# A third weight chunk ahead of x, smaller first loads, and small matmuls among the rows of a one-core decoder layer

## The chip, the cores and the metric

The kernel runs on one core of a Trainium2 chip. The metric is the device time of one execution in microseconds (us), the median over the runs shown. TensorE does the matrix products, VectorE (DVE in the profile), ScalarE (ACT) and GpSimd (POOL) the elementwise work; SyncE (SP) issues most of the loads. Each engine takes its instructions strictly in the order in which they stand in its own list and waits on semaphores for the others.

## The reference

One layer of a decoder trunk on 256 tokens of width 1024, with 256 memory tokens, all in float32:

```
h = rms_norm(x, norm_mix_g)                       # mean of squares, sqrt, reciprocal, gain
x = x + hybrid_mixer(h, ...)                      # h @ w_in -> conv module (u), NSA attention (q, kc, vc, ...), gates; @ w_out
h = rms_norm(x, norm_x_g)
x = x + cross_attention(h, mem, xq_w, xkv_w, xo_w)
#   q = h @ wq; k, v = split(mem @ wkv); p = softmax(q k^T / sqrt(256)) over 4 heads; o = (p v) @ wo
h = rms_norm(x, norm_ffn_g)
x = x + swiglu(h, ffn_in_w, ffn_out_w)
return rms_norm(x, final_norm_g)
```

The keys of the cross-attention, `mem @ wkv`, need only `mem`. So the kernel computes them first, while `x` is still being loaded and normalised.

## The kernel before

**Tiles.** Activations are held transposed, as 8 blocks of 128 channels by 256 tokens. The weights come in chunks of 256 columns (1 MB), each loaded in two halves of 512 KB. `k0` to `k3` are the four chunks of the cross-attention's keys, `u0` to `u7` the conv module's, then `kc`, `vc`, `q0` and so on; `xq0` to `xq3` and `xo0` to `xo3` are the cross-attention's query and output chunks, `f0` to `f21` those of the FFN. In the names of the profile the chunk's number is left out: `k_0h` is the high part of half 0 of some k chunk.

**Splitting.** A float32 operand is split in two parts that TensorE multiplies fast: `split` (L174 and after) lets ScalarE copy the half to a rounded high part (L184) and VectorE subtract that from it to get the low part (L186). From `u1` to the gates' first chunk GpSimd does the subtraction instead. `part` (L301 to L304) does the same for activations: `memh`, `meml` from `mem_t`; `hh`, `hl` from `hf`; `kxh`, `kxl` from a finished k bank.

**Matmuls.** `rows` (L248 to L262) multiplies one half of a chunk: three rows of 8 matmuls, 128x128 by 128x256 each, namely high weights by high activations, high by low, low by high. A chunk so takes 48 matmuls of L259. Only `k0` is multiplied in plain float32 (`whole`, L289), straight from the loads.

**The start.** After 8 warm-up products (L364), TensorE does `k0`, then `k1`, then the norm of x: `rooted_all` (L343 to L351) multiplies the squares of x, folded to two blocks on VectorE (L399), by a matrix of ones (L347, the bank `rn`); ScalarE takes the root (L349), VectorE the reciprocal (L350), then eight products give `hf` (L405) in four pairs, and each pair is split (`part`) to `hh`, `hl`. Then the rest of `k2`, `k3` and the u chunks follow. Loads are issued by SP in the order of the calls: `k0`, `k1`, x in two halves, two tables (`cpt`, `ppt`), `k2`, `k3`, `u0`; `mem_t` is loaded from ScalarE's queue.

**What sets the order.** A scheduler with a model of the engines puts the instructions of each engine in order ahead of the run. The kernel bounds it by marks: `first[name]` (L178) says after which instruction a chunk may be split, `in_line` (L240) chains rows of TensorE, and from `xq0` to the xo chunks `in_turn` (from L1038) writes the order out by hand.

**Cross-attention.** The scores' scale is the norm of the new x, which `rnorm(acc1, "2", 256.0)` (L329 to L341, bank `rn`) makes from two small products with 2 columns (L333), a root and a reciprocal. It is called ahead of `in_turn` (L980), its result `r16` is first used behind the first scores (`xscores(0)`, L1010, L1013).

**The small matmul.** `settle` (L244 to L246) multiplies 32 columns of an activation by 256 of it into a bank that the next chunk's first row starts afresh, so its product is thrown away. Before, it stands once, ahead of `f4`.

Of the kernel before, what the change touches and what calls it, by code (L numbers as in the profile page):

```python
# [12 lines left out]
ALU = mybir.AluOpType  # L13
# [84 lines left out]
def tile_hybrid_block(  # L98
# [56 lines left out]
    def aux(name, shape, tag, bufs):  # L155
        return axp.tile(shape, F32, tag=tag, name=name, bufs=bufs)
# [47 lines left out]
    def ahead(name, slot):  # L204

        w = held[name] = long(f"{name}w", slot, (P, NB, 256))
        if name == "k0":
            for i in range(4):
                nc.sync.dma_start(w[:, 2 * i:2 * i + 2], w0[i])
            return  # L210
        for i in range(2):
            nc.sync.dma_start(w[:, 4 * i:4 * i + 4], wst[CHUNK_AT[name]][:, 4 * i:4 * i + 4])
# [31 lines left out]
    def settle(o, x):  # L244

        nc.tensor.matmul(o[0:32], lhsT=x[:, 0:32], rhs=x, start=True, stop=True)  # L246

# [81 lines left out]
    def rnorm(sq, name, scale=1.0, tag="o"):  # L329

        ps = aux(f"rn_{name}", [P, 2, 2], tag, 1)
        for tb in range(2):
            nc.tensor.matmul(ps[:, tb], lhsT=sq[:, tb * P:tb * P + P], rhs=ones[:, 0:2], start=tb == 0, stop=tb == 1)  # L333
        r = small(f"r_{name}", [P, 2], tag="rnat", bufs=2)
        if name == "l":

            nc.vector.tensor_scalar(out=r, in0=ps[:, :, 0], scalar1=EPS, scalar2=None, op0=ALU.add)
            return newton(r, name)
        root = nc.scalar.activation(r, ps[:, :, 0], AF.Sqrt, scale=scale, bias=eps256 if scale != 1.0 else eps1)
        first[name] = root, nc.vector.reciprocal(r, r)  # L340
        return r  # L341
# [31 lines left out]
    for i in range(4):  # L373
        nc.scalar.dma_start(mem_t[:, 2 * i:2 * i + 2], memt[i])
    ahead("k0", 10)
    ahead("k1", 14)
    for i in range(2):
        nc.sync.dma_start(xt_t[:, 4 * i:4 * i + 4], xt[:, 4 * i:4 * i + 4])
    nc.sync.dma_start(cpt, cp)
    nc.sync.dma_start(ppt, pp)  # L380
    for name, slot in (("k2", 12), ("k3", 11), ("u0", 13)):
        ahead(name, slot)
# [8 lines left out]
    for i in range(2):  # L391
        hs = slice(4 * i, 4 * i + 4)
        part(memh[:, hs], meml[:, hs], mem_t[:, hs])
# [7 lines left out]
    first["k2_1"] = first["1"]  # L401
# [8 lines left out]
    for name, i in (("u0_0", 2), ("u0_1", 3), ("u1_0", 3), ("u1_1", 3)):  # L410
        first[name] = first[f"x{i}"]
# [57 lines left out]
    for j in range(NB):  # L469
        ps = gemm(f"u{j}", h)  # L470
        sg = small(f"sg{j}", [P, S], tag="sg", bufs=3)
        act = nc.scalar.activation(sg, ps[:, 1], AF.Sigmoid)
        vec = nc.vector.tensor_tensor(out=vt[j][:, PAD:], in0=ps[:, 0], in1=sg, op=ALU.mult)
        convolve(13 * (j > 0), (0, 1, 1, 1, 1, 0, 1, 1)[j], act, vec)
# [505 lines left out]
    r16 = rnorm(acc1, "2", 256.0)  # L980
    xmax, xneg, xsum = (small(n, [P, 4, 2]) for n in ("xmax", "xneg", "xsum"))
    oxh, oxl, pxh, pxl = longs(("oxh", "oxl", "pxh", "pxl"), (13, 9, 11, 12))
    px, queries = [None] * 4, [None] * 4
# [18 lines left out]
    def xscores(j):  # L1002
# [7 lines left out]
        nc.vector.scalar_tensor_tensor(out=xneg[:, j], in0=xmax[:, j], scalar=-1.0, in1=r16, op0=ALU.mult, op1=ALU.mult)  # L1010
        px[j] = small(f"px{j}", [P, 2, S], tag="vt", bufs=4)
        for qb in range(2):
            nc.scalar.activation(px[j][:, qb], s_ps[:, qb], AF.Exp, scale=r16[:, qb:qb + 1], bias=xneg[:, j, qb:qb + 1],  # L1013
                                 accum_out=xsum[:, j, qb:qb + 1])
# [25 lines left out]
    def in_turn():  # L1040
# [12 lines left out]
        some(qs[1], 3)  # L1053
        xscores(0)
        some(qs[1], 4)
# [20 lines left out]
        xo(2, 0)  # L1076
# [136 lines left out]
    homes.append(gf[:, 2:4])  # L1213
    for j in range(NF):
        ps = bank(f"ps_f{j}")
        if j == 4:
            settle(ps[:, 0], fg[:, 0, 0])
        gemm(f"f{j}", (fg[:, 0], fg[:, 1]), ps=ps)
# [279 lines left out]
```

## Time and profile before

| | us |
|---|---|
| median of 3 runs | 531.47 (531.02 to 531.73) |
| the profiled execution's own time | 532.03 |
| its span, first to last instruction | 530.0 |
| TensorE busy | 522.3 |
| VectorE, ScalarE, GpSimd busy | 433.9, 343.7, 156.0 |

The profiled execution lies 0.56 us above the median, and 2.03 us of its time lie outside the span. The mean granted clock of TensorE was 0.997. In the timeline a row is a group of instructions in a row on one engine with one form: its start, the time from its first instruction's start to its last one's end, engine, line, operation, output from inputs, and the count; in brackets the idle time ahead of it and what ended it. Matmuls overlap, so the end of a row lies past the start of the next one, and the spacing of matmuls is the difference of two rows' starts divided by the number of matmuls between them. A float32 product of L347, L289 or the warm-up shows as two records in the trace and stands once in the order.

### The profile page before, as it was taken

How to read it: one execution, taken by the hardware profiler on the slowest of the kernel's cores; microseconds unless marked ns; L12 is line 12 of the kernel's file. 1: busy time of each engine (PE TensorE's matmuls, PEld its weight loads, DVE VectorE, ACT ScalarE, POOL GpSimd, SP SyncE). 2: the span in 40 equal slices, each digit the busy share in tenths (PEclk: the TensorE clock that was granted, in tenths of full speed). 3: DMA queues.
4: the chain of work that ended last, by engine and by line, in shares of the span. 5: the costliest groups of instructions: out<-in, count | busy, mean ns of one | idle time of the engine just before them, and what ended most of it. 6: DMA issues, size and time to landing. Idle time of an engine off the chain costs nothing.

```text
span 530.0 us, 11121 instructions
## 1 busy us (share of the span) xinstructions
PE 522.3 (99%) x4316; PEld 504.8 (95%) x4316; DVE 433.9 (82%) x871; ACT 343.7 (65%) x599; POOL 156.0 (29%) x110
## 2 busy tenths in 40 slices
PE   9999999999999999999999999999999999999995
PEld 8999999999999999999999999999999999988884
DVE  4868999899978898975869676697889888878985
ACT  4685466787656888789446664665556665657553
POOL 0069999999961200200004000330000000000001
PEclk9999999999999999999999999999999999999998
DMA  8927954664355544347765643847765567455622
GB/s 309 416 98 267 350 185 161 202 216 160 121 182 177 178 141 135 105 147 213 233 205 171 235 153 119 236 167 258 218 199 198 198 233 226 157 137 173 220 88 80
DMA packets 30740, 101.55 MB, mean 192 GB/s; under 512 B 3296, under 2 KB 5856, under 8 KB 30304
## 3 DMA queue, kind: packets, MB, share of 16 engines
q1 hardware_dynamic: 29104, 96.99, 54.0%
q0 software_dynamic: 864, 2.62, 3.1%
q10 hardware_dynamic: 720, 1.23, 0.6%
q8 instruction: 34, 0.56, 0.5%
q14 instruction: 18, 0.15, 0.1%
HBM read 99.59 MB, written 1.25 MB: 190 GB/s over the span
## 4 chain that ended last, share of the span: by engine, by line
PE 60%; DVE 1%; ACT 0%; issue 0%; ACTq 0%; DVEq 0%
PE ps_f L259 23%; PE fo L1254 6%; PE ps_xo L259 4%; PE ps_v L259 4%; PE ps_pw L259 4%; PE ps_wo L259 4%; PE ps_xq L259 4%; PE m L1254 4%; PE xs L989 1%; PE xo_ps L989 1%; PE o L819 1%; PE pt_a L798 1%; PE s L753 1%; PE o L816 1%; PE pt_b L798 0%; PE o L810 0%
## 5 line engine op out<-in xcount | busy, mean ns | idle before, releaser
L437 DVE SCALAR_TENSOR_TENSOR yp<-vt,ppt,yp 128x256 f32<-128x256 f32 x204 | 81.6, 480 | 0.2
L259 PE MATMUL ps_f<-g,f_1h 128*128 128x256 f32 x352 | 44.4, 277 | 0.0
L259 PE MATMUL ps_f<-g,f_0h 128*128 128x256 f32 x352 | 43.8, 277 | 0.0
L259 PEld LDWEIGHTS ps_f<-g,f_1h 128*128 128x128 f32 x352 | 42.1, 188 | 0.1
L259 PEld LDWEIGHTS ps_f<-g,f_0h 128*128 128x128 f32 x352 | 41.8, 188 | 0.0
L184 ACT ACTIVATE f_0h<-f 128x1024 fp32r<-128x1024 f32 x22 | 23.3, 1057 | 16.8 <-issue 5.7
L186 DVE TENSOR_TENSOR f_1l<-f,f_1h 128x1024 fp32r<-128x1024 f32 x22 | 27.4, 1248 | 6.8 <-ACT f_1h L184 5.9
L184 ACT ACTIVATE f_1h<-f 128x1024 fp32r<-128x1024 f32 x22 | 23.3, 1060 | 14.3 <-PE ps_f L259 10.6
L186 DVE TENSOR_TENSOR f_0l<-f,f_0h 128x1024 fp32r<-128x1024 f32 x22 | 26.7, 1212 | 1.7 <-ACT f_0h L184 1.7
L186 POOL TENSOR_TENSOR u_0l<-u,u_0h 128x1024 fp32r<-128x1024 f32 x7 | 17.4, 2479 | 30.4 <-DVE kt L523 30.4
L259 PE MATMUL ps_f<-g,f_0l 128*128 128x256 f32 x176 | 23.9, 277 | 0.0
L259 PE MATMUL ps_f<-g,f_1l 128*128 128x256 f32 x176 | 23.7, 277 | 0.0
L259 PEld LDWEIGHTS ps_f<-g,f_0l 128*128 128x128 f32 x176 | 21.9, 188 | 0.0
L1220 DVE TENSOR_TENSOR ab<-ps_f,r 128x512 f32<-128x512 f32 x22 | 15.1, 689 | 8.3 <-PE ps_f L259 8.3
L259 PEld LDWEIGHTS ps_f<-g,f_1l 128*128 128x128 f32 x176 | 21.7, 188 | 0.0
L773 ACT ACTIVATE p<-p,mins 128x256 f32<-128x256 f32 x32 | 15.9, 502 | 8.4 <-DVE mins L758 8.4
L1138 POOL DMA_DIRECT2D spare<-in_wfo_dram x1 | 0.9, 866 | 65.1 <-DVE ab L1220 65.1
L186 POOL TENSOR_TENSOR u_1l<-u,u_1h 128x1024 fp32r<-128x1024 f32 x7 | 17.9, 2560 | 0.0
L449 POOL TENSOR_TENSOR yt<-yt,vw 128x512 f32<-128x512 f32 x13 | 17.1, 1312 | 0.0
L1222 ACT ACTIVATE sl<-ab 128x256 f32<-128x256 f32 x22 | 9.1, 417 | 11.1 <-DVE ab L1220 11.1
L1296 POOL TENSOR_TENSOR x<-y,gf 128x512 f32<-128x512 f32 x2 | 2.6, 1298 | 46.1 <-issue 46.1
L259 PE MATMUL ps_u<-hh,u_0h 128*128 128x256 f32 x128 | 16.1, 276 | 0.0
(614 smaller groups left out, 1632.1 us busy)
## 6 DMA issues: line engine op xcount, KB each, us to landing
f<-in_wst_dram SPq DMA_DIRECT2D x44, 512.0 KB, 4.3
fo<-in_wfo_dram SPq DMA_DIRECT2D x16, 512.0 KB, 3.5
u<-in_wst_dram SPq DMA_DIRECT2D x14, 512.0 KB, 7.9
q<-in_wst_dram SPq DMA_DIRECT2D x8, 512.0 KB, 4.1
ga<-in_wst_dram SPq DMA_DIRECT2D x8, 512.0 KB, 3.5
gc<-in_wst_dram SPq DMA_DIRECT2D x8, 512.0 KB, 3.7
v<-in_wst_dram SPq DMA_DIRECT2D x8, 512.0 KB, 5.8
pw<-in_wst_dram SPq DMA_DIRECT2D x8, 512.0 KB, 4.8
```

Source lines behind the costliest of these rows:

```text
L184: copy = nc.scalar.activation(hi, w, AF.Copy)
L186: splits[name] = copy, eng.tensor_tensor(out=lo, in0=w, in1=f(hi[:]), op=ALU.subtract)
L259: mm = nc.tensor.matmul(ps[:, b], lhsT=lhsT, rhs=rhs, start=row + b + kb == 0, stop=kb == NB - 1 and row == 2 and b == 1)
L437: nc.vector.scalar_tensor_tensor(out=out[:, i] if t == ts[-1] else acc[i], in0=v, scalar=w, in1=acc[i], op0=ALU.mult, op1=ALU.add)
L449: nc.gpsimd.tensor_tensor(out=yt[:, 0:2], in0=yt[:, 0:2], in1=pr, op=ALU.add)
L753: nc.tensor.matmul(s1, lhsT=qh(hd, 1), rhs=t[:, g].rearrange("p b t -> p (b t)"), start=i == 0, stop=i == 1)
L773: exp.append(nc.scalar.activation(p1[k][:, br], p1[k][:, br], AF.Exp, scale=-1.0, bias=mins[:, hd, 1, br:br + 1], accum_out=sums[:, hd, 1, ...
L798: mm = nc.tensor.transpose(ps[:, i], src, ident)
L989: mm = nc.tensor.matmul(o, lhsT=lhsT, rhs=rhs, start=n == 0, stop=n == len(order) - 1)
L1220: scaled[:] = [nc.vector.tensor_tensor(out=ab, in0=ps, in1=rf.unsqueeze(1).to_broadcast([P, 2, S]), op=ALU.mult)]
L1222: silu = nc.scalar.activation(sl, ab[:, 0], AF.Silu)
L1254: mm = nc.tensor.matmul(o, lhsT=a[x], rhs=b[w], start=start and n == 0, stop=stop and n == 2)
```

## The change

Five edits. (1) The first quarter of `mem_t` and of `k0`'s weights is each loaded as two pieces of 128 KB instead of one of 256 KB; the second half of `memh`, `meml` is split in two steps. (2) `k2` is loaded ahead of x instead of behind the tables, and its second half no longer waits for the norm's root; `u0`'s first half may be split one pair of `hf` earlier. (3) A small matmul stands among the rows of `k3`, into the bank of `u1`. (4) `r16` is made right ahead of `xscores(0)`; its bank is wider, and a small matmul goes into its second half behind the scores. (5) A small matmul stands behind the first row of `xo2`, and the one ahead of `f4` moves eight matmuls into `f3`. `settled` is `settle` chained in the line of rows.

```diff
         if name == "k0":
-            for i in range(4):
+            for k in range(2):
+                nc.sync.dma_start(w[:, k], w0[0, :, k])
+            for i in range(1, 4):
                 nc.sync.dma_start(w[:, 2 * i:2 * i + 2], w0[i])
...
+    def settled(o, x):
+
+        with in_line():
+            last[:] = [nc.tensor.matmul(o[0:32], lhsT=x[:, 0:32], rhs=x, start=True, stop=True)]
...
-    def rnorm(sq, name, scale=1.0, tag="o"):
-
-        ps = aux(f"rn_{name}", [P, 2, 2], tag, 1)
-        for tb in range(2):
-            nc.tensor.matmul(ps[:, tb], lhsT=sq[:, tb * P:tb * P + P], rhs=ones[:, 0:2], start=tb == 0, stop=tb == 1)
+    def rnorm(sq, name, scale=1.0, tag="o", beside=None):
+
+        ps = aux(f"rn_{name}", [P, 2, S], tag, 1)
+        with in_line() if beside is not None else ExitStack():
+            for tb in range(2):
+                mm = nc.tensor.matmul(ps[:, 0, 2 * tb:2 * tb + 2], lhsT=sq[:, tb * P:tb * P + P], rhs=ones[:, 0:2], start=tb == 0, stop=tb == 1)
+        if beside is not None:
+            last[:] = [mm]
+            beside.append(ps[:, 1])
+        ps = ps[:, 0, 0:4].rearrange("p (t c) -> p t c", t=2)
...
-    for i in range(4):
+    for k in range(2):
+        nc.scalar.dma_start(mem_t[:, k], memt[0, :, k])
+    for i in range(1, 4):
         nc.scalar.dma_start(mem_t[:, 2 * i:2 * i + 2], memt[i])
     ahead("k0", 10)
     ahead("k1", 14)
+    ahead("k2", 12)
...
-    for name, slot in (("k2", 12), ("k3", 11), ("u0", 13)):
+    for name, slot in (("k3", 11), ("u0", 13)):
         ahead(name, slot)
...
-    for i in range(2):
-        hs = slice(4 * i, 4 * i + 4)
+    for hs in (slice(0, 4), slice(4, 6), slice(6, 8)):
         part(memh[:, hs], meml[:, hs], mem_t[:, hs])
...
-    first["k2_1"] = first["1"]
...
-    for name, i in (("u0_0", 2), ("u0_1", 3), ("u1_0", 3), ("u1_1", 3)):
+    for name, i in (("u0_0", 1), ("u0_1", 3), ("u1_0", 3), ("u1_1", 3)):
...
-        ps = gemm(f"u{j}", h)
+        ps = bank(f"ps_u{j}")
+        if j == 1:
+            settle(ps[:, 0], memh[:, 0])
+        gemm(f"u{j}", h, ps=ps)
...
-    r16 = rnorm(acc1, "2", 256.0)
...
         some(qs[1], 3)
+        r16.append(rnorm(acc1, "2", 256.0, beside=free))
         xscores(0)
+        settled(free[0], xg[0][:, 0])
...
-        xo(2, 0)
+        half_xo2 = rows(pss[2], halved("xo2", 0), (oxh, oxl), 0)
+        next(half_xo2)
+        settled(pss[3][:, 0], oxh[:, 0])
+        for _ in half_xo2:
+            pass
...
+    banks = []
     for j in range(NF):
-        ps = bank(f"ps_f{j}")
-        if j == 4:
-            settle(ps[:, 0], fg[:, 0, 0])
-        gemm(f"f{j}", (fg[:, 0], fg[:, 1]), ps=ps)
+        ps = banks.pop() if banks else bank(f"ps_f{j}")
+        for i in range(2):
+            for n, _ in enumerate(rows(ps, halved(f"f{j}", i), (fg[:, 0], fg[:, 1]), i, line=j == 3)):
+                if j == 3 and i + n == 0:
+                    banks.append(bank("ps_f4"))
+                    settled(banks[0][:, 0], fg[:, 0, 0])
```

In the changed kernel the lines are shifted: L259 is L266, `rooted_all`'s products L347 are L359, the root L349 is L361, `part` L303 is L310, the reciprocal L350 is L362, L405 is L418, and the small matmul is L248 (`settle`) or L253 (`settled`).

TensorE's order at the start, before (ps_k_140 is k1's bank, ps_k_225 that of k2, ps_k_284 that of k3, rn_203 the norm of x):

```order
8 L259 MATMUL ps_k_140<-memh,k_1l 128x256 x8
9 L347 MATMUL rn_203<-xtsq,ones 128x256 x2
10 L259 MATMUL ps_k_225<-memh,k_0h 128x256 x8
11 L259 MATMUL ps_k_225<-meml,k_0h 128x256 x8
12 L259 MATMUL ps_k_225<-memh,k_0l 128x256 x8
13 L259 MATMUL ps_k_225<-memh,k_1h 128x256 x8
14 L259 MATMUL ps_k_225<-meml,k_1h 128x256 x8
15 L259 MATMUL ps_k_284<-memh,k_0h 128x256 x8
16 L259 MATMUL ps_k_284<-meml,k_0h 128x256 x8
17 L259 MATMUL ps_k_225<-memh,k_1l 128x256 x8
18 L259 MATMUL ps_k_284<-memh,k_0l 128x256 x8
19 L259 MATMUL ps_k_284<-memh,k_1h 128x256 x8
```

And now (ps_k_229 is k2's bank, ps_k_288 that of k3, ps_u_419 that of u1, ps_u_359 that of u0):

```order
14 L266 MATMUL ps_k_229<-memh,k_1l 128x256 x8
15 L359 MATMUL rn_207<-xtsq,ones 128x256 x2
16 L266 MATMUL ps_k_288<-memh,k_0h 128x256 x8
17 L266 MATMUL ps_k_288<-meml,k_0h 128x256 x8
18 L266 MATMUL ps_k_288<-memh,k_0l 128x256 x8
19 L248 MATMUL ps_u_419<-memh 32x256
20 L266 MATMUL ps_k_288<-memh,k_1h 128x256 x8
21 L266 MATMUL ps_k_288<-meml,k_1h 128x256 x8
22 L266 MATMUL ps_u_359<-hh,u_0h 128x256 x10
23 L266 MATMUL ps_k_288<-memh,k_1l 128x256 x8
```

All 48 matmuls of k2 now stand ahead of the norm. Between the norm and the first row that needs the second half of k3 stood 72 matmuls; now 24 and the small one stand there. From that row on, 69 matmuls stand ahead of the row with `u_1l` of u0 (8 and 8 of k3, 10, 8 of k3, 6, 8 and 16 of u0, 5 of u1).

ScalarE's order around the root, before (r_206 is the norm's root):

```order
9 L184 ACTIVATE k_0h<-k2w 128x1024
10 L303 ACTIVATE kxh<-ps_k_140 128x512
11 L349 ACTIVATE r_206<-rn_203,eps_t 128x256
12 L184 ACTIVATE k_1h<-k2w 128x1024
13 L184 ACTIVATE k_0h<-k3w 128x1024
14 L303 ACTIVATE hh<-hf 128x512
15 L184 ACTIVATE k_1h<-k3w 128x1024
```

And now:

```order
14 L411 ACTIVATE xtsq<-xtsq 128x1024
15 L184 ACTIVATE k_0h<-k3w 128x1024
16 L361 ACTIVATE r_210<-rn_207,eps_t 128x256
17 L310 ACTIVATE hh<-hf 128x512
18 L184 ACTIVATE k_1h<-k3w 128x1024
19 L310 ACTIVATE hh<-hf 128x512
20 L184 ACTIVATE u_0h<-u0w 128x1024
```

The split of k3's second half stands behind the first split of `hf` in both. VectorE's order behind the reciprocal is now `hf` eight times, `hh`, `k_1l` of k3, `hh`, `u_0l`, `hh`, the clearing of `kt`, `hh`, `kxl`, `u_1l`; the low parts of k2 and of k3's first half, which stood between the reciprocal and `hf`, are ahead of it.

TensorE at the first scores, before (rn_3965 is the bank of `r16`, ps_xq_4046 that of xq1, xs the scores):

```order
475 L259 MATMUL ps_xq_4046<-gh_3682,xq_0h 128x256 x2
476 L333 MATMUL rn_3965<-ones,acc_3684 128x2 x2
477 L259 MATMUL ps_xq_4046<-gh_3682,xq_0h 128x256 x6
478 L259 MATMUL ps_xq_4046<-gl_3683,xq_0h 128x256 x8
479 L259 MATMUL ps_xq_4046<-gh_3682,xq_0l 128x256 x8
480 L989 MATMUL xs_4077<-kxh,xqh_4042 128x256 x4
```

And now:

```order
475 L266 MATMUL ps_xq_4045<-gh_3687,xq_0h 128x256 x8
476 L266 MATMUL ps_xq_4045<-gl_3688,xq_0h 128x256 x8
477 L266 MATMUL ps_xq_4045<-gh_3687,xq_0l 128x256 x8
478 L341 MATMUL rn_4076<-ones,acc_3689 128x2 x2
479 L1004 MATMUL xs_4082<-kxh,xqh_4041 128x256 x4
480 L1004 MATMUL xs_4082<-kxl,xqh_4041 128x256 x4
481 L1004 MATMUL xs_4082<-kxh,xql_4042 128x256 x4
482 L253 MATMUL rn_4076<-gh_3687 32x256
```

The two small products have moved 22 matmuls back, and the new small matmul follows the scores.

More of the change, by code (lines that the diff above doesn't have):

```diff
@@ L977, in tile_hybrid_block @@
     x1, xg, acc1 = residual(by_halves([f"wo{j}" for j in range(4)], (yh, yl)), xr, PP_GX, "1", (0, 1, 6))
-    r16 = rnorm(acc1, "2", 256.0)
     xmax, xneg, xsum = (small(n, [P, 4, 2]) for n in ("xmax", "xneg", "xsum"))
     oxh, oxl, pxh, pxl = longs(("oxh", "oxl", "pxh", "pxl"), (13, 9, 11, 12))
-    px, queries = [None] * 4, [None] * 4
+    px, queries, r16, free = [None] * 4, [None] * 4, [], []
     def turned_in(order):
@@ L1009, in xscores @@
         nc.vector.tensor_reduce(out=xmax[:, j], in_=s_ps, axis=AX.X, op=ALU.max)
-        nc.vector.scalar_tensor_tensor(out=xneg[:, j], in0=xmax[:, j], scalar=-1.0, in1=r16, op0=ALU.mult, op1=ALU.mult)
+        nc.vector.scalar_tensor_tensor(out=xneg[:, j], in0=xmax[:, j], scalar=-1.0, in1=r16[0], op0=ALU.mult, op1=ALU.mult)
         px[j] = small(f"px{j}", [P, 2, S], tag="vt", bufs=4)
         for qb in range(2):
-            nc.scalar.activation(px[j][:, qb], s_ps[:, qb], AF.Exp, scale=r16[:, qb:qb + 1], bias=xneg[:, j, qb:qb + 1],
+            nc.scalar.activation(px[j][:, qb], s_ps[:, qb], AF.Exp, scale=r16[0][:, qb:qb + 1], bias=xneg[:, j, qb:qb + 1],
                                  accum_out=xsum[:, j, qb:qb + 1])
```

## The prediction

> **What bounds the kernel now.** I read the page first: busy time, granted clock, and the chain that ended last.
>
> ```profile
> PE 522.3 (99%) x4316; PEld 504.8 (95%) x4316; DVE 433.9 (82%) x871; ACT 343.7 (65%) x599; POOL 156.0 (29%) x110
> PEclk9999999999999999999999999999999999999998
> PE 60%; DVE 1%; ACT 0%; issue 0%; ACTq 0%; DVEq 0%
> ```
>
> TensorE is busy all through, so only three things can move the time: matmuls added, TensorE's waits, and the spacing of its matmuls. The waits of TensorE were read next:
>
> ```profile
> PE warm L364 <- DVE eps_t L167: 1.1, 1, 1.1
> PE rn L347 <- DVE xtsq L399: 0.5, 1, 0.5
> ```
>
> One wait of any size is left behind the warm-up, at the norm of x. Next TensorE's timeline at the start (start, duration, then what, with its count):
>
> ```profile
> 12.35 1.11 PE L259 MATMUL ps_k<-meml,k_0h 128*128 128x256 f32 x8
> ...
> 16.12 1.10 PE L259 MATMUL ps_k<-memh,k_1l 128*128 128x256 f32 x8
> 17.70 1.10 PE L347 MATMUL rn<-xtsq,ones 128*128 128x256 f32 x4 [0.47 <-DVE xtsq L399]
> 18.45 1.28 PE L259 MATMUL ps_k<-memh,k_0h 128*128 128x256 f32 x8
> 19.57 1.07 PE L259 MATMUL ps_k<-meml,k_0h 128*128 128x256 f32 x8
> ...
> 26.83 1.07 PE L259 MATMUL ps_k<-memh,k_1h 128*128 128x256 f32 x8
> ...
> 35.89 1.07 PE L259 MATMUL ps_u<-hh,u_1l 128*128 128x256 f32 x8
> ...
> 40.43 1.98 PE L259 MATMUL ps_u<-hh,u_0h 128*128 128x256 f32 x16
> ```
>
> Two things are to be seen. The same matmul comes in two spacings: (16.12 - 12.35)/32 = 117.8 ns in k1, and (26.83 - 19.57)/64 = 113.4 ns behind the norm, 4.4 ns apart, at the same granted clock. And k1 would have ended at 16.12 + 8 x 0.1178 = 17.06, so the norm's start at 17.70 loses 0.64 us.
>
> **The smaller first pieces.** k0's matmuls start when the warm-up ends and not when a load lands (no wait for a DMA is among TensorE's). Earlier bytes change nothing: 0.
>
> **k2 ahead of the norm: what it removes.** The norm then stands behind k2, at R = 17.06 + 48 x 0.1178 = 22.71; with nothing small between them I let k2 keep k1's spacing. Will x be there? These are ScalarE's rows at the start:
>
> ```profile
> 13.21 1.06 ACT L397 ACTIVATE xtsq<-xtsq 128x1024 f32<-128x1024 f32 x1 [0.43 <-DMA xtsq<-in_xt_dram]
> 14.51 1.06 ACT L397 ACTIVATE xtsq<-xtsq 128x1024 f32<-128x1024 f32 x1 [0.23 <-DMA xtsq<-in_xt_dram]
> ...
> 16.65 1.06 ACT L184 ACTIVATE k_0h<-k2w 128x1024 fp32r<-128x1024 f32 x1 [1.08 <-DMA k2w<-in_wst_dram]
> ...
> 18.84 0.48 ACT L349 ACTIVATE r<-rn,eps_t 128x256 f32<-128x256 f32 x1 [0.65 <-PE rn L347]
> ...
> 24.26 0.63 ACT L303 ACTIVATE hh<-hf 128x512 fp32r<-128x512 f32 x1 [3.05 <-DVE hf L405]
> 24.80 1.04 ACT L184 ACTIVATE k_1h<-k3w 128x1024 fp32r<-128x1024 f32 x1
> ```
>
> And VectorE's:
>
> ```profile
> 15.60 1.95 DVE L399 TENSOR_TENSOR xtsq<-xtsq 128x1024 f32<-128x1024 f32 x2 [1.45 <-ACT xtsq L397]
> ...
> 19.49 1.74 DVE L350 RECIPROCAL r<-r 128x256 f32<-128x256 f32 x1
> ...
> 23.35 3.25 DVE L405 SCALAR_TENSOR_TENSOR hf<-xtsq,ppt,r 128x256 f32<-128x256 f32 x8
> 26.52 0.68 DVE L304 TENSOR_TENSOR hh<-hf,hh 128x512 fp32r<-128x512 f32 x1
> ...
> 28.26 1.28 DVE L304 TENSOR_TENSOR hh<-hf,hh 128x512 fp32r<-128x512 f32 x2
> 29.46 1.22 DVE L186 TENSOR_TENSOR u_0l<-u0w,u_0h 128x1024 fp32r<-128x1024 f32 x1
> ...
> 30.74 0.62 DVE L304 TENSOR_TENSOR hh<-hf,hh 128x512 fp32r<-128x512 f32 x1
> ...
> 31.88 2.84 DVE L186 TENSOR_TENSOR u_1l<-u0w,u_1h 128x1024 fp32r<-128x1024 f32 x1
> ```
>
> x takes k2's old place in SP's queue. k2's first half landed at about 16.6 (it released the split at 16.65). x's second half landed 1.3 behind its first (14.51 against 13.21), so now at about 17.9; with the square and the fold (1.06 and 1.95) x is ready by about 21, ahead of 22.71. The stall of 0.64 goes; the spacing gives back 48 x 0.0044 = 0.21.
>
> **What it uncovers, first stall.** The norm's chain used to run beside 72 matmuls. Now 24 and a small one stand between the norm and the first row that needs k3's second half. That split waits on ScalarE behind the first split of `hf`, which waits for VectorE. From the norm's start, by the rows above: the reciprocal ends at 19.49 + 1.74 - 17.70 = 3.53; `hf` follows at once, since the low parts that stood there are ahead of it now; `hh` on ScalarE follows the start of `hf` by 24.26 - 23.35 = 0.91, at 4.44; the split of k3 comes 0.54 later (24.80 - 24.26) and takes 1.04: R + 6.02. TensorE gets there after the norm's 0.75 (18.45 - 17.70), its next eight 1.12 (19.57 - 18.45), 16 x 0.1134 = 1.81 and the small matmul 0.12: R + 3.80. **Stall 2.22 us.** Every duration has a row; the least I can see is 1.9 (the root and `hf` a little sooner), the most 2.5.
>
> **Second stall.** The 69 matmuls up to u0's `u_1l` take 7.82, so TensorE asks for it at R + 6.02 + 7.82 = R + 13.84. VectorE makes it last of a row of work: from `hf` at R + 3.53, 3.17 to the first `hh` (26.52 - 23.35), 1.74 for that and k3's low part (28.26 - 26.52), 0.60 for `hh` (half of 29.46 - 28.26), 1.28 for `u_0l` and the clearing (30.74 - 29.46), 0.60 and 1.14 (31.88 - 30.74) for `hh`, `hh` and `kxl`: it starts at R + 12.06. In before it took 2.84, beside GpSimd's first split:
>
> ```profile
> 30.81 2.83 POOL L186 TENSOR_TENSOR u_0l<-u,u_0h 128x1024 fp32r<-128x1024 f32 x1 [30.36 <-DVE kt L523]
> ```
>
> The same subtraction alone (29.46) took 1.22. GpSimd is released by the clearing of `kt`, which stands at the same distance ahead of `u_1l` now, so they overlap again and I take 2.84: R + 14.90. **Stall 1.06 us**; with 1.22 it would be nothing. So 0 to 1.06, near the upper end.
>
> **The sum of the start.** Then 51 matmuls (8 of `u_1l`, 43 of u1), 5.78, to u2's first: 3.80 + 2.22 + 7.82 + 1.06 + 5.78 = 20.68, or 43.39 against 40.43: **+2.96**. Without both stalls it would be -0.32. Nothing later gives it back, since TensorE has no other wait to lose it in.
>
> **The small matmuls.** The late rows of TensorE:
>
> ```profile
> 294.02 1.10 PE L259 MATMUL ps_xq<-gl,xq_0h 128*128 128x256 f32 x8
> 294.97 1.10 PE L259 MATMUL ps_xq<-gh,xq_0l 128*128 128x256 f32 x8
> ...
> 304.43 0.60 PE L1026 MATMUL xpt<-cpt,px 128*128 128x128 f32 x4
> ...
> 305.79 1.07 PE L259 MATMUL ps_xq<-gl,xq_1h 128*128 128x256 f32 x8
> 306.70 1.07 PE L259 MATMUL ps_xq<-gh,xq_1l 128*128 128x256 f32 x8
> ...
> 327.83 1.11 PE L259 MATMUL ps_xo<-oxl,xo_0h 128*128 128x256 f32 x8
> 328.78 1.10 PE L259 MATMUL ps_xo<-oxh,xo_0l 128*128 128x256 f32 x8
> ...
> 351.62 0.59 PE L347 MATMUL rn<-acc,ones 128*128 128x256 f32 x2
> ...
> 370.06 0.28 PE L246 MATMUL ps_f<-g 128*32 128x256 f32 x1
> 370.18 1.98 PE L259 MATMUL ps_f<-g,f_0h 128*128 128x256 f32 x16
> 371.99 1.07 PE L259 MATMUL ps_f<-g,f_0l 128*128 128x256 f32 x8
> ```
>
> Rows lie 0.95 apart (slow) at 294 and 328, 0.91 (fast) at 306; the change of pace falls at groups of other matmuls. The one small matmul, at 370.06, stands where slow turns fast ((371.99 - 370.18)/16 = 113.1 ns) and costs 0.12. One case is thin; I reckon three in four that another does the same.
>
> - At the first scores: 22 matmuls of xq1 get ahead of the norm's two products and stay fast, -0.10. The 60 behind the scores, to 304.43, would gain 0.26 less 0.12, but `xql` from VectorE may hold the next scores: together -0.05 (-0.25 to +0.12). `r16` itself is used after the scores, so its move puts nothing late.
> - The stretches to 327 change pace at each `xpt` group and may now do so the other way round: +0.10 (+-0.3).
> - In xo2: 202 matmuls from 327.83 to 351.62 lose 4.4 ns each, 0.89. But the norm at 351.62 waits for GpSimd's sum of squares, whose last row is this:
>
> ```profile
> 349.36 1.87 POOL L971 TENSOR_TENSOR acc<-acc,s_xo 128x256 f32<-128x256 f32 x2 [2.03 <-ACT s_xo L962]
> ```
>
> It ended at 351.23. If it doesn't move, only 0.39 is gained; I take 0.64, less 0.12 for the matmul itself, and half of 0.40 for the 92 behind the norm: 0.72, times three quarters -0.55 (-1.2 to +0.12).
> - In f3: 40 matmuls, -0.18; the small one is moved, not added.
>
> Together -0.68. [...]
>
> **The sum.** 2.96 - 0.68 = +2.28 on the profiled execution (532.03 to 534.3) and on the median, 0.56 lower: **533.8**. Its own range, from the terms' bounds, is 532.9 to 534.6.
>
> **The rivals.**
>
> - *The norm's chain is hidden (faster).* If `hh` on ScalarE were ready at R + 2.2 and not R + 4.44, neither stall would appear: -0.32 - 0.68, 530.5. For it: before, the chain cost TensorE nothing, and DVE's work between reciprocal and `hf` is gone. Against: root, reciprocal and two `hf` are 3.5 us of work with rows, and 3.8 us lie above them. 0.13.
> - *Only the first stall.* If GpSimd starts later than VectorE's `u_1l`, that takes 1.22: 2.28 - 1.06, 532.7. 0.15.
> - *The small matmuls change no spacing*: 2.96 + 2 x 0.12, 534.7. For it: other groups keep the pace (351.62 slow on both sides). 0.14.
> - *The u stretch goes slow* behind the stalls: 24 + 384 matmuls to the first group of another kind, 1.8 more: 535.6. 0.08.
> - *The clock drops in the stall*: 30 matmuls at twice 113.4 ns add 3.4: 537.2. PEclk shows none. [...] 0.02.
>
> **How the numbers follow.** The forecast has 0.48. The measurement tells 0.2%, 1.06 us, from no change. The first rival lies at that edge: 0.08 faster, 0.05 same; the second too: 0.07 same, 0.08 slower; all else is slower. Faster 0.08, same 0.12, slower 0.80. The range 532.0 to 535.6 leaves out the first rival, the clock's, and the upper half of the u stretch, some 0.2.
>
> **What would show it.** Right: in the waits of TensorE, none at the norm, about 2.2 us at `k_1h` of k3 behind ACT, about 1 us at `u_1l` behind DVE; u2's first row near 43.4; rows 0.91 apart from the second of xo2 to the FFN. Wrong: no wait at `k_1h`, u2 near 40.1, or waits later in the program that have grown.

## The result and the profile after

The changed kernel takes 539.89 us (median of 5, 536.75 to 541.16) against 531.47 us (530.97 to 531.73): 1.0145 times as long, with a 95% interval of 1.0115 to 1.0175. Slower was forecast, but 533.8 with a range up to 535.6. The profiled execution is the median one, 539.89 us with a span of 538.1, so 7.86 us above the profiled one of before and 8.1 in the span.

The waits of TensorE in the changed kernel, with the total, the times and the longest:

```profile
PE ps_k L266 <- ACT k_1h L184: 2.0, 1, 2.0
PE warm L376 <- DVE eps_t L167: 1.1, 1, 1.1
PE ps_k L296 <- DMA mem_t<-in_memt_dram: 1.0, 1, 1.0
PE ps_u L266 <- DVE u_1l L186: 0.8, 1, 0.8
```

The two stalls of the prediction are there, 2.0 and 0.8 us where 2.22 and 1.06 were worked out, and the norm's wait is gone. A third wait, for `mem_t` in k0, was not forecast. TensorE's timeline at the start of the changed kernel:

```profile
4.64 1.98 PE L296 MATMUL ps_k<-mem_t,k0w 128*128 128x256 f32 x8
7.62 5.42 PE L296 MATMUL ps_k<-mem_t,k0w 128*128 128x256 f32 x24 [1.00 <-DMA mem_t<-in_memt_dram]
12.69 1.29 PE L266 MATMUL ps_k<-memh,k_0h 128*128 128x256 f32 x8
...
24.18 1.02 PE L359 MATMUL rn<-xtsq,ones 128*128 128x256 f32 x4
...
30.08 1.20 PE L266 MATMUL ps_k<-memh,k_1h 128*128 128x256 f32 x8 [2.02 <-ACT k_1h L184]
...
38.96 1.19 PE L266 MATMUL ps_u<-hh,u_1l 128*128 128x256 f32 x8 [0.77 <-DVE u_1l L186]
...
44.86 1.98 PE L266 MATMUL ps_u<-hh,u_0h 128*128 128x256 f32 x16
```

For comparison, four rows of before that were not shown (k0, the first of k1, the transposes ahead of f3, the first of the FFN's output):

```profile
4.37 7.20 PE L289 MATMUL ps_k<-mem_t,k0w 128*128 128x256 f32 x32
11.22 1.29 PE L259 MATMUL ps_k<-memh,k_0h 128*128 128x256 f32 x8
...
362.66 1.91 PE L1102 MATMUL fo<-cpt,x 128*128 128x128 f32 x16
...
468.10 0.39 PE L1254 MATMUL fo<-fo_0h,uh 128*128 128x512 f32 x1
```

k1 begins 12.69 - 11.22 = 1.47 us later: k0 starts 4.64 - 4.37 = 0.27 later, 1.00 is the wait, and 0.20 is left for k0's own products. u2 begins 44.86 - 40.43 = 4.43 later, so 2.96 us of delay were added between the two: the very sum of the prediction for k2's move. Now the late part of the changed kernel:

```profile
331.21 1.17 PE L266 MATMUL ps_xo<-oxh,xo_0h 128*128 128x256 f32 x8
332.22 0.28 PE L253 MATMUL ps_xo<-oxh 128*32 128x256 f32 x1
332.33 1.07 PE L266 MATMUL ps_xo<-oxl,xo_0h 128*128 128x256 f32 x8
333.24 1.07 PE L266 MATMUL ps_xo<-oxh,xo_0l 128*128 128x256 f32 x8
...
366.18 1.91 PE L1123 MATMUL fo<-cpt,x 128*128 128x128 f32 x16
367.84 1.19 PE L266 MATMUL ps_f<-g,f_0h 128*128 128x256 f32 x8
368.87 0.28 PE L253 MATMUL ps_f<-g 128*32 128x256 f32 x1
368.99 1.11 PE L266 MATMUL ps_f<-g,f_0h 128*128 128x256 f32 x8
369.93 1.11 PE L266 MATMUL ps_f<-g,f_0l 128*128 128x256 f32 x8
...
475.46 0.40 PE L1278 MATMUL fo<-fo_0h,uh 128*128 128x512 f32 x1
```

Behind the small matmul in xo2 rows lie 0.91 apart, and the delay shrinks to 366.18 - 362.66 = 3.52. Behind the one in f3 they still lie 0.94 apart: there it did not turn the spacing. The delay grows to 475.46 - 468.10 = 7.36 by the end of the FFN's first products, 3.84 us more. That stretch alone is half of the loss. The output rows add 0.13 (the last store is issued 533.88 - 526.39 = 7.49 later), and the span's end lies another 0.6 later still, behind that store:

```profile
526.39 0.37 ACTq L1355 DMA_DIRECT2D out_dram<-x  x1
```

```profile
533.88 0.37 ACTq L1379 DMA_DIRECT2D out_dram<-x  x1
```

That fast rows follow a small matmul doesn't yet say that it made them fast. The last four matmuls ahead of the one in xo2 and of the one in f3:

```profile
331.76 0.62 PE L266 MATMUL ps_xo<-oxh,xo_0h 128*128 128x256 f32 x4
...
368.40 0.64 PE L266 MATMUL ps_f<-g,f_0h 128*128 128x256 f32 x4
```

From their starts to those of the small matmuls they are (332.22 - 331.76)/4 = 115 and (368.87 - 368.40)/4 = 118 ns apart; the trace's starts, which are in whole ns, give 113 to 114 and 117 to 118. So in xo2 the spacing was fast before the small matmul came, and in f3 it stayed slow behind it.

### The profile page after: what moved, and what is told of

It reads as the page before. It is cut to its first block, busy times and chain, and to the rows that moved or that the text cites. A ratio compares the mean times of both kernels' runs of the same rounds, so it can differ in the third digit from the quotient of the medians.

```text
span 538.1 us, 11135 instructions
## 1 busy us (share of the span) xinstructions
PE 526.4 (98%) x4319; PEld 508.2 (94%) x4319; DVE 433.1 (80%) x872; ACT 344.3 (64%) x600; POOL 156.2 (29%) x110
## 4 chain that ended last, share of the span: by engine, by line
PE 60%; DVE 1%; ACT 0%; issue 0%; ACTq 0%; DVEq 0%
PE ps_f L266 23%; PE fo L1278 6%; PE ps_v L266 4%; PE ps_pw L266 4%; PE ps_xo L266 4%; PE ps_wo L266 4%; PE ps_xq L266 4%; PE m L1278 4%; PE xs L1004 1%; PE xo_ps L1004 1%; PE o L835 1%; PE pt_a L814 1%; PE s L769 1%; PE o L832 1%; PE pt_b L814 0%; PE o L826 0%
## 5 line engine op out<-in xcount | busy, mean ns | idle before, releaser
L266 PE MATMUL ps_f<-g,f_1h 128*128 128x256 f32 x352 | 45.5, 281 | 0.0
L266 PE MATMUL ps_f<-g,f_0h 128*128 128x256 f32 x352 | 45.0, 281 | 0.0
L266 PEld LDWEIGHTS ps_f<-g,f_1h 128*128 128x128 f32 x352 | 43.1, 189 | 0.1
L266 PEld LDWEIGHTS ps_f<-g,f_0h 128*128 128x128 f32 x352 | 42.9, 189 | 0.0
L266 PE MATMUL ps_f<-g,f_0l 128*128 128x256 f32 x176 | 24.5, 281 | 0.0
L266 PE MATMUL ps_f<-g,f_1l 128*128 128x256 f32 x176 | 24.2, 281 | 0.0
L266 PEld LDWEIGHTS ps_f<-g,f_0l 128*128 128x128 f32 x176 | 22.3, 189 | 0.0
L266 PEld LDWEIGHTS ps_f<-g,f_1l 128*128 128x128 f32 x176 | 22.2, 189 | 0.0
L774 DVE CUSTOM_DVE_ANT_0 p<-s,nb 128x256 f32<-128x256 f32 x32 | 11.8, 421 | 5.5 <-PE s L769 5.5
L266 PE MATMUL ps_u<-hh,u_0h 128*128 128x256 f32 x128 | 16.1, 276 | 0.0
```

The source lines that it names most:

```text
L266: mm = nc.tensor.matmul(ps[:, b], lhsT=lhsT, rhs=rhs, start=row + b + kb == 0, stop=kb == NB - 1 and row == 2 and b == 1)
L774: nc.vector.tensor_tensor_reduce(out=p1[k][:, br], in0=s1[:, br], in1=nbp[:, k], scale=1.0, scalar=3e38, op0=ALU.add, op1=ALU.min, accum_o ...
```

## The experiments

Times of a kernel are compared with runs of the kernel before on the same chip; "heap" is a group of executions whose times lie close together.

**Undoing one part of the change.** a1 puts the first loads back, a2 the small matmul ahead of f4, a3 the place of k2 with its marks; a4 is the kernel before with only the late part.

```diff
# a1: on the changed kernel
-            for k in range(2):
-                nc.sync.dma_start(w[:, k], w0[0, :, k])
-            for i in range(1, 4):
+            for i in range(4):
                 nc.sync.dma_start(w[:, 2 * i:2 * i + 2], w0[i])
...
# a2: on the changed kernel
+        ps = bank(f"ps_f{j}")
+        if j == 4:
+            settle(ps[:, 0], fg[:, 0, 0])
+        gemm(f"f{j}", (fg[:, 0], fg[:, 1]), ps=ps)
...
# a3: on the changed kernel
-    ahead("k2", 12)
...
-    for name, slot in (("k3", 11), ("u0", 13)):
+    for name, slot in (("k2", 12), ("k3", 11), ("u0", 13)):
...
# a4: on the kernel before
-    r16 = rnorm(acc1, "2", 256.0)
+        r16.append(rnorm(acc1, "2", 256.0, beside=free))
         xscores(0)
+        settled(free[0], xg[0][:, 0])
...
+        settled(pss[3][:, 0], oxh[:, 0])
```

> The changed kernel with the first loads in 256 KB pieces as before, all else changed. Theory (the parts add up): TensorE's wait of 1.0 us for mem_t goes and k0 ends near 11.2 instead of 12.7, so 1.4 to 1.5 us come off the changed kernel's 539.9, about 538.4; the stalls at k_1h and u_1l stay at 2.0 and 0.8. Rival (the later norm is what makes k0 late, through the queue order of k2): k0 still ends near 12.7 and nothing comes off.

Measured: 539.17 us, 538.68 to 542.02. The wait for `mem_t` is gone, but k0 still ends at 12.5. By itself this is inconclusive; why k0 ends late without a wait is told below. The expected 538.4 was missed for a second reason: in its profile the stall at `k_1h` is 2.3 us and none is left at `u_1l`, because the granted clock falls to 0.50 behind the first (see b2), and the u chunks run at 117.8 ns too, which the prediction had as a rival at 0.08.

> The changed kernel with the small matmul back ahead of f4 instead of among f3's rows. Theory (the small matmul in f3 does not turn the FFN's spacing): f4 to f21 run at 113.4 ns instead of 117.8, 864 matmuls by 4.4 ns or 3.8 us less, about 536.1, and the executions lie within 1 us of each other again instead of spreading over 4.4. Rival (the FFN's spacing follows from when it starts, which has shifted by 4 us): still 117.8, still 539.9, still spread.

Measured: 537.18 us, 536.46 to 538.5: 2.7 less than the changed kernel, and one heap. f4 to f21 run fast in its profile, so the rival (the start's delay sets the pace) falls and the theory holds in kind. In size it falls short, 2.7 for 3.8 and executions 2.0 apart instead of 1: its start varies by the wait for `mem_t` (1.6 us in its profile) and by the clock (see b2).

> The changed kernel with k2 loaded behind the tables again, its old mark and u0's old mark. Theory: the two stalls of 2.0 and 0.8 us go and the wait of 0.5 at the norm comes back, 2.9 us less, about 537.0 (if the FFN's spacing stays as in the changed kernel). Rival (x is late anyway, since the smaller first loads push everything back): the norm's wait grows to over 1.5 and less than 2 us are gained.

Measured: 536.83 us, but in two heaps: three executions at 531.86 to 533.09 and nine at 535.86 to 537.41. The profiled one is of the lower heap (532.43), with f4 to f21 fast. The upper heap is where the theory put it (537.0). So with k2 back in its place, and the small first loads and k3's small matmul still there, the same program runs the FFN at one or the other spacing, by execution, three fast in twelve.

> The kernel before with the late part alone: r16 moved ahead of the first scores with the small matmul behind them, and the one in xo2; start and f4 as before. Theory: the xo2 one turns 202 and more matmuls from 117.8 to 113.4 ns, the scores' part is about nothing: 0.5 to 1.1 us less than before, 530.4 to 531.0. Rival (the spacing turns only by chance, by what came ahead): within 0.3 us of before or slower.

Measured: 531.36 us against 531.89, ratio 0.9992 (0.9976 to 1.0008): no difference that can be told, so the expected 0.5 to 1.1 us are not shown, though xo2 is fast in its profile as in the changed kernel. The other profiles say why little is to be won. Of the twelve without a small matmul in xo2, six have it fast all the same (b1, b3, c1, c2, e5, e6) and six slow; these are rows of e6:

```profile
327.86 1.07 PE L259 MATMUL ps_xo<-oxl,xo_0h 128*128 128x256 f32 x8
328.77 1.07 PE L259 MATMUL ps_xo<-oxh,xo_0l 128*128 128x256 f32 x8
```

In all six profiles with one (the changed kernel, a1 to a4, e1) the four matmuls ahead of it are fast already. What these six have in common ahead of xo2 is edit (4): the rows in front of the first `xpt` group are fast (113 ns; slow at the same place in the other twelve up to the next scores), and in 17 of the 18 profiles the spacing changes at each of the four `xpt` groups, so that it comes out fast in xo2.

**One part alone, on the kernel before.** b0 is the kernel before once more, for its profile. b1, b2 and b3 make edits (1), (2) and the f3 part of (5) of the change, as the diff above shows them.

> The kernel before, unchanged, for its profile beside the others'. In the runs so far k0 ended near 12.5 us even with the first loads as before, against 11.2 in the first profile. Theory (the landing of the first loads differs from execution to execution, whatever their size): k0 ends anywhere from 11.2 to 12.7 here as well, and since the norm waits 0.6 us for x, most of it is lost in that wait: the time stays within 0.6 us of 531.5. Rival (the small pieces delay them): k0 ends near 11.2.

Measured: 532.07 us, 530.86 to 533.96. k0 ends at 12.51 here with the first loads of before. The row of windows says why, first the old profile, then this one (stretch, its length, then for each engine the busy time and the number of instructions, TensorE first):

```profile
4.60:8.00 3.40, 3.40 (x17) 2.81 (x16) 1.23 (x1) 1.06 (x1) 0.00 (x0) 1.00 0.99 371
```

```profile
4.60:8.00 3.40, 3.40 (x13) 2.82 (x12) 1.23 (x1) 1.06 (x1) 0.00 (x0) 1.00 1.00 354
```

TensorE is busy all through in both, but gets 13 products done and not 17: some k0 products follow each other at 427 ns, twice the usual 216. In the twelve other profiles with the first loads of `mem_t` as before, k1 begins anywhere from 11.22 to 12.65. So part of the 1.47 us (at most the 0.47 outside the wait) was not the change's.

> The kernel before with the smaller first loads alone. Theory (they do nothing of their own): the same time as before within 0.5 us, k0 ends where it does in the kernel before on the same chip. Rival (they cost 1.0 to 1.5 us by TensorE's wait for mem_t, 0.6 of it swallowed by the norm's wait): 0.5 to 1.0 us slower.

Measured: 533.5 us against 531.59, ratio 1.0029 (1.0012 to 1.0046), 0.6 to 2.4 us slower, with this wait:

```profile
PE ps_k L291 <- DMA mem_t<-in_memt_dram: 1.5, 1, 1.5
```

The theory that the smaller pieces do nothing falls. k1 begins at 13.38, later than in any profile with the old pieces; the norm is then at 19.22 without a wait of its own, so of the 2.16 against the first profile 0.64 were hidden there (17.70).

> The kernel before with k2 loaded ahead of x alone (and its mark taken off, u0's moved), no small matmul. Theory: stalls of 2.0 to 2.3 us at k_1h and up to 1.0 at u_1l, the norm's wait gone: 2.5 to 3.3 us slower, about 534.4. Rival (the stalls come from the smaller loads and the small matmul beside it): under 1.5 us slower.

Measured: 535.77 us, ratio 1.007 (1.0051 to 1.009), 3.7 us slower. The stall is there, and something behind it. TensorE's wait, and the windows (the figure behind the five engines is PEclk, the granted clock as a share of full speed):

```profile
PE ps_k L259 <- ACT k_1h L184: 2.4, 1, 2.4
```

```profile
26.80:29.00 2.20, 0.02 (x1) 0.00 (x0) 2.20 (x6) 1.44 (x2) 0.00 (x0) 0.99 0.04 17
29.00:31.00 2.00, 1.81 (x8) 1.81 (x9) 2.00 (x5) 2.00 (x4) 0.00 (x0) 0.50 0.00 0
31.00:33.00 2.00, 2.00 (x14) 2.00 (x13) 2.00 (x3) 2.00 (x5) 0.00 (x0) 0.66 0.00 0
33.00:35.00 2.00, 2.00 (x20) 2.00 (x20) 2.00 (x5) 2.00 (x4) 0.89 (x1) 1.00 0.04 12
```

Behind the stall the granted clock is 0.50 for over 3 us: 8 and 14 products in two stretches of 2 us, where 20 fit at 1.00. The same dip shows in the profiles of a1 and a2, and not in that of the changed kernel itself. That is the rival to which the prediction gave 0.02. The mean granted clock of each execution says the same: it lies below 0.996 in 14 of the 23 executions of these four kernels, and in none of the 142 of the other kernels here. From `k_1h`'s first product to u2's first, 120 products, it takes 15.18 us here, 15.35 in a2 and 14.78 in the changed kernel, which has the second stall and no dip: the dip costs 0.4 to 0.6 us more than the stall that it swallows. Stalls of 2.0 (a2) to 2.4 us were enough for the dip in three profiles of four.

> The kernel before with the small matmul moved from ahead of f4 into f3 alone. Theory (there it turns the FFN's spacing only in some executions): two heaps of times, one within 0.3 us of before, one 3.8 to 4.2 us above it, with more executions in the upper one. Rival (the spread of the changed kernel comes from its start): one heap, within 0.5 us of before.

Measured: two heaps again, five executions at 530.88 to 532.13 and six at 535.57 to 536.40 (one at 533.76). The theory holds in so far as the FFN's spacing differs by execution, with everything else as before. But in the profiles it isn't the small matmul that turns the rows. The profiled execution is of the lower heap (532.13), and the rows ahead of the small matmul are fast there already:

```profile
365.16 0.62 PE L264 MATMUL ps_f<-g,f_0h 128*128 128x256 f32 x4
365.62 0.28 PE L251 MATMUL ps_f<-g 128*32 128x256 f32 x1
365.73 1.07 PE L264 MATMUL ps_f<-g,f_0h 128*128 128x256 f32 x8
```

The same holds in a3's profile, which is of the lower heap too; in the changed kernel and in a1 the rows are slow ahead of it and slow behind it. In none of the four did the small matmul behind the first eight matmuls of f3 change anything. The rows come out of the `fo` transposes ahead of f3 fast or slow, by execution (fast also in c1, e1 and e5, slow in the eleven other profiles), and without a small matmul that works they stay so to the FFN's end (in the changed kernel still 0.94 us for 8 products at 474.51; also c4).

**Where the stall goes, and the small matmul's place.** c1 is b2 without the mark that holds back k3's second half. c2 is b3 with another place; c3 and c4 change the one matmul ahead of f4.

```diff
# c1: on b2
-        if i == 2:
-            first["k3_1"] = first["x0"][0], vec
...
# c2: on b3
-                if j == 3 and i + n == 0:
+                if j == 3 and (i, n) == (0, 2):
...
# c3: on the kernel before
             settle(ps[:, 0], fg[:, 0, 0])
+            settle(ps[:, 0], fg[:, 0, 0])
...
# c4: on the kernel before
-        if j == 4:
-            settle(ps[:, 0], fg[:, 0, 0])
```

> The kernel before with k2 ahead of x and, besides, the mark taken off that holds the split of k3's second half behind the first hh: ScalarE and VectorE make it ahead of the norm's root. Theory (the stall is k3's second half behind the norm's chain; its cover is back when 46 matmuls of k3 can run beside the chain; and the granted clock falls to 0.5 only behind a stall over 2 us): no wait at k_1h, waits under 1.2 us in all up to u2, PEclk 1.00 there, and a time 2.5 to 4 us under that of k2 ahead alone (535.8), 531.5 to 533. Rival (the norm's chain itself is what TensorE waits for, whoever stands behind it): the stall moves to u_0h with the same 2 us, the clock falls there too, and the time stays at 535 to 536.

Measured: 533.83 us against 532.27, ratio 1.0014 (0.9998 to 1.003). TensorE's waits, beside that of the warm-up:

```profile
PE ps_u L259 <- ACT u_0h L184: 0.4, 1, 0.4
...
PE ps_u L259 <- DVE u_0l L186: 0.2, 1, 0.2
```

No wait at `k_1h`, 0.6 us behind it, and the granted clock is 1.00 from 29 to 35 us. The stall was the norm's chain without cover, and most of it goes with the cover back. The time is a little above the expected 531.5 to 533, and by the ratio 0.1 less to 1.6 us more than before: k2 ahead of x, even mended, was not shown to win anything.

> The kernel before with the small matmul in f3 behind 24 matmuls instead of 8. Theory (the draw is made by standing close behind the 16 plain products of the fo transposes): the FFN turns fast in every execution, one heap at 531 to 532. Rival (any place within a half's rows draws): two heaps again, 4 us apart.

Measured: 531.87 us against 532.27, none above 534.18. In the profile the rows are 118 ns apart ahead of the small matmul and 113 behind it. The upper heap is gone: here the small matmul does work.

> The kernel before with two small matmuls in a row ahead of f4. Theory (one such matmul toggles the spacing): two toggle back, the FFN stays at 117.8 ns and the time is 3.8 to 4.2 us above before. Rival (it sets the spacing to the fast one, from either): the same time as before plus 0.1.

Measured: 532.28 us, as before. The small matmul doesn't toggle; a second one leaves the fast spacing alone. The single one ahead of `f4` finds slow rows in eight other profiles, and in all eight the rows behind it are fast.

> The kernel before without any small matmul in the FFN. Theory (the pace that f1 to f3 have lasts to the end): all executions with f1 to f3 slow stay slow, 3.7 to 4.1 us above before, one heap around 535.6. Rival (the pace is drawn anew by each chunk): close to before, or spread evenly.

Measured: 536.0 us, 535.13 to 536.16, ratio 1.0058 (1.0039 to 1.0077). Without it the FFN stays slow to the end in all six. So the one ahead of f4 was worth 3.7 us by the medians (3.1 by the ratio), and the change put that at stake.

**What was left.** e1 is the kernel before with the small matmuls alone (f3's behind 24), e2 has only the smaller pieces of `mem_t`, e5 fills the stall of b2, e6 has only the one among k3's rows.

```diff
# e5: on b2 (e6: on the kernel before, with range(1))
+        ps = bank(f"ps_u{j}")
+        if j == 1:
+            for _ in range(16):
+                settle(ps[:, 0], memh[:, 0])
+        gemm(f"u{j}", h, ps=ps)
...
# e2: on the kernel before
+    for k in range(2):
+        nc.scalar.dma_start(mem_t[:, k], memt[0, :, k])
-    for i in range(4):
+    for i in range(1, 4):
         nc.scalar.dma_start(mem_t[:, 2 * i:2 * i + 2], memt[i])
...
# e1: on the changed kernel, first loads and k2 as before
-                if j == 3 and i + n == 0:
+                if j == 3 and (i, n) == (0, 2):
```

> The kernel before with k2 ahead of x, and 16 small matmuls into u1's bank between k3's rows where TensorE would stall. They do no work that is used. Theory (the stall is idle time, and idle time is what halves the granted clock): the stall shrinks from 2.4 to about 0.5 us, PEclk stays 1.00 behind it, and the time is 1.0 to 1.5 us under k2 ahead alone, 534.3 to 534.8. Rival (the clock falls for what the engine does behind the stall, or the fill delays k_1h): no gain, 535.8 or more.

Measured: 534.83 us against 531.92, ratio 1.0051 (1.0035 to 1.0068). The wait and two stretches of its windows:

```profile
PE ps_k L259 <- ACT k_1h L184: 0.6, 1, 0.6
```

```profile
29.00:31.00 2.00, 2.00 (x20) 2.00 (x19) 2.00 (x4) 2.00 (x4) 0.00 (x0) 1.00 0.00 0
31.00:33.00 2.00, 2.00 (x20) 2.00 (x20) 2.00 (x3) 2.00 (x3) 0.00 (x0) 1.00 0.04 8
```

With the idle time filled by products that are thrown away, the clock stays at 1.00, and the loss against before is 2.7 us and not 3.7. All six executions have a mean clock of 0.999, against 0.993 to 0.998 in b2. So with k2 ahead the clock fell to 0.50 behind 2.4 us of idle time (b2) and stayed at 1.00 behind 0.6 (here). Not all of the 1.0 us is the dip's: the fill leaves no second stall either, and the 120 products from `k_1h`'s first on take 13.7 us. The two ratios' intervals just overlap; the windows and the clocks are the clearer evidence.

> The kernel before with mem_t's first quarter in two pieces and k0's weights as before (nine first loads). Theory (the fifth load of a queue and the more numerous packets of both queues share the blame): about half of the 1.5 us that both cost, 0.5 to 1.0 slower than before. Rival (mem_t's piece is the one TensorE waits for, so it is all of it): 1.2 to 1.7 slower, with TensorE's wait for mem_t over 1 us. Second rival (k0's pieces do it): no wait for mem_t and no difference.

Measured: 532.59 us against 531.92, ratio 1.0026 (1.0012 to 1.004), with this wait:

```profile
PE ps_k L289 <- DMA mem_t<-in_memt_dram: 0.7, 1, 0.7
```

`mem_t`'s pieces alone cost 1.4 us (0.6 to 2.1), about what both cost together (1.5); the interval doesn't rule out the theory's 0.5 to 1.0, but the second rival, no wait at all, falls. ScalarE splits the first half of `mem_t` as soon as it has landed, 2.6 us later than before (first row before, second e2):

```profile
5.58 1.06 ACT L303 ACTIVATE memh<-mem_t 128x1024 fp32r<-128x1024 f32 x1 [1.45 <-DMA mem_t<-in_memt_dram]
```

```profile
8.22 1.06 ACT L303 ACTIVATE memh<-mem_t 128x1024 fp32r<-128x1024 f32 x1 [2.53 <-DMA mem_t<-in_memt_dram]
```

ScalarE's queue issues the four loads from 0.74 to 2.60 before and the five from 0.74 to 4.16 here, so a later issue may be part of it; that it is the whole cause isn't shown.

> The kernel before with the one small matmul among k3's rows alone. Theory (in some executions of the kernel before, the rows from k2 to the end of the u chunks keep k1's 117.8 ns, 432 matmuls or 1.9 us; this matmul sets the fast spacing): the executions at 533 to 534.5 go, the fastest ones stay where they are plus 0.1. Rival (that heap has another cause): the same spread as before.

Measured: 531.87 us, 530.48 to 532.28, against 531.92, ratio 0.9987 (0.9973 to 1.0002); none of 11 executions above 532.3, where 6 of 29 of before lie above 533. That fits the theory without proving it. That the u chunks do draw is seen in the profile of c2, where nothing ahead of them differs from before; rows of k2 lie 0.94 apart where before had 0.91:

```profile
19.49 1.10 PE L264 MATMUL ps_k<-meml,k_0h 128*128 128x256 f32 x8
20.43 1.10 PE L264 MATMUL ps_k<-memh,k_0l 128*128 128x256 f32 x8
```

> The kernel before with the four small matmuls of the change and the moved norm, and nothing of its start: first loads and k2 as before, and the one of the FFN in f3 behind 24 matmuls, where no execution failed. Theory (the small matmuls set the fast spacing wherever they do not stand close behind the plain products): the heap of executions at 533 to 534.5 that the kernel before has (u0 to u7 slow) goes, and 0.5 to 1 us come off in xo2: median 530.8 to 531.5, faster than before by 0.2 to 0.3% on the same chip. Rival (they only shift where the slow stretches lie): the same median and the same spread as before.

Measured: 531.87 us against 531.92, ratio 0.9993 (0.9982 to 1.0005), ten of eleven at 531.09 to 532.33 and one at 533.57. That one has the profile, with the small matmul at 26.17:

```profile
25.23 1.10 PE L264 MATMUL ps_k<-memh,k_1l 128*128 128x256 f32 x8
26.17 0.28 PE L246 MATMUL ps_u<-memh 128*32 128x256 f32 x1
26.29 1.10 PE L264 MATMUL ps_k<-memh,k_0l 128*128 128x256 f32 x8
27.23 1.11 PE L264 MATMUL ps_k<-memh,k_1h 128*128 128x256 f32 x8
```

Rows are 0.94 apart on both sides: among k3's rows it can fail. In the five other profiles with one there (the changed kernel, a1 to a3, e6) the rows ahead of it are fast already, so no run shows it working at that place. No version was shown to beat the kernel before.

## Why the prediction was wrong

The direction was right, and so was the mechanism named for it. The size was wrong, by 6 us, and three steps failed; a fourth came out near its forecast for another reason than the one given.

- **The norm's chain without cover** held. The two stalls came out at 2.0 and 0.8 for 2.22 and 1.06, and the 2.96 us between k1 and u2 were met to the hundredth, which owes something to chance: the first stall ends 5.90 behind the norm instead of 6.02, and the rows behind the stalls are 0.12 longer. The cover experiment (c1) shows the cause. The low parts on VectorE beside GpSimd took what they took before:

```profile
36.07 2.83 DVE L186 TENSOR_TENSOR u_1l<-u0w,u_1h 128x1024 fp32r<-128x1024 f32 x1
```

- **"In f3: 40 matmuls, -0.18; the small one is moved, not added"** failed, and is the largest error. The step counted the rows ahead of the new place and took for granted that the small matmul works at any place. Behind the first eight matmuls of f3 it changed the spacing in none of four profiles (b3), while ahead of `f4` it turned slow rows fast in nine of nine and behind 24 in the one that came to it slow (c2). So the FFN kept the spacing that the transposes ahead of f3 had left: slow in seven of twelve executions of b3 at most and in nine of twelve of a3, at 3.7 us each (c4). In the profiled execution it cost 3.84 us. The prediction had said "one case is thin" and given three chances in four, but used them for the gain in xo2 only, not for the gain that the kernel already had.
- **"Earlier bytes change nothing: 0"** failed. The step looked at the gain, saw none, and gave no bound on the other side. The pieces delay the second quarter of `mem_t`, and TensorE waits for it: about 1.5 us alone (b1), and there part was still hidden at the norm, whose wait k2's move takes away. In the profiled execution k1 is 1.47 later: 1.00 by the wait, the rest by the draw at the start that b0 shows.
- **"The clock drops in the stall", 0.02**, was far too low: it fell to 0.50 in three of the four profiles that have the stall together with k2 ahead and no fill. The rival had 3.4 us, from 30 products at twice the spacing; no run shows that 30. By rows the dip costs 0.4 to 0.6 us: some 14 to 16 products run slow, and they also swallow the second stall (no wait at `u_1l` in a1, a2 and b2). In the profiled execution it did not happen, so it explains part of the spread and not the 7.86.
- **"In xo2", -0.55** came out at -0.89, but not by the small matmul there, which finds fast rows in every profile (a4). The prediction had the reason in its own list: the stretches ahead "change pace at each `xpt` group and may now do so the other way round". They do, since the rows behind the first scores are now fast. That edit (4) made them so is argued from the rows in six profiles; no run has it alone. Of the twelve profiles without that edit, six have the same fast rows in xo2. The delay falls from 330.86 - 326.45 = 4.41 at the last transposes of the probabilities to 3.52:

```profile
330.86 0.60 PE L1041 MATMUL xpt<-cpt,px 128*128 128x128 f32 x4
```

```profile
326.45 0.60 PE L1026 MATMUL xpt<-cpt,px 128*128 128x128 f32 x4
```

- **The scores and the stretches up to xo2** together: the delay is 4.43 at u2 and 4.41 at those transposes: nothing, as forecast (-0.05 + 0.10).

The sum in the profiled execution is then 1.47 + 2.96 - 0.02 - 0.89 + 3.84 + 0.13 + 0.6 = 8.09, the span's 8.1; the last 0.6, behind the last store's issue, has no cause shown. By the ratios, the parts alone give 1.5 (b1), 3.7 (b2) and 3.1 (c4, in the executions that come slow out of the transposes), 8.3 where the whole change cost 7.7, each with an interval of some 1 us to either side.

What stays open: why a slow spacing stays slow behind the small matmul at eight matmuls of f3 and among k3's rows (e1), and not ahead of `f4` or behind 24; and what decides the spacing behind the `fo` transposes. Without a small matmul in the FFN it was slow in all six executions (c4), with one in f3 fast in five of twelve (b3), so the program may have a part in it. That the place in f3 stands close behind the plain transposes was argued; e1's failure, with no such products near, speaks against it as the whole reason.

## What to carry to other kernels

A step that is moved takes its present gain along: ask what hangs on it where it stands, and put that at stake in the range, not only what it may win at the new place. A load or a norm that is made early is worth what waits for it; count what stands between it and the next dependent row, for that is the cover that the move takes away. Before a step gets the credit for what follows it, look at the rows ahead of it: they may have been so already. And when a kernel's executions spread after a change that shouldn't touch its variance, look for two heaps: a median then tells how often, not how much.

## What the runs showed of the hardware

- The same 128x128 by 128x256 product follows itself at 113.4 or at 117.8 ns over hundreds of products, and one 32-column product of 0.12 us ahead of `f4` sets the faster pace for the next hundred us (536.0 us without it, 532.3 on the same chip with it). Two in a row do the same as one (532.28 us, c3). At two other places (the changed kernel and a1 in f3, e1 in k3) a slow pace stayed slow behind it (118 ns in the changed kernel, 0.94 us a row of 8 in e1).
- The pace changed at transposes: in 17 of 18 profiles at each of the cross-attention's four groups of four (128x128), fast to slow or slow to fast, and in 9 of 18 at the 16 ahead of f3.
- A stall of 2.0 to 2.4 us of TensorE was followed, in three profiles of four, by over 3 us at a granted clock of 0.50; with the stall filled down to 0.6 us it stayed at 1.00, and all six executions had a mean of 0.999.
- At the start some of k0's products follow each other at 427 ns and not at 216 (b0), for a time that differs by execution: k1 begins between 11.22 (before) and 12.65 us with the same loads. PEclk reads 1.00 there all the same.
- Two pieces of 128 KB in place of the first 256 KB of `mem_t` made TensorE wait 0.7 us for the piece behind them (e2); with k0's weights in such pieces too it was 0.7 (a3) to 1.6 us (a2).
